# Splitting two pairs' projection weights early and reloading them as parts

## The chip, the cores and the metric

The kernel runs on one core of a Trainium2 chip. The time is that of one execution on the device, in microseconds (us); of several runs the median is given. One more execution was taken with the hardware profiler: its trace gives every instruction's start and duration on the engines PE (TensorE: matmuls and transposes), DVE (VectorE), ACT (ScalarE), POOL (GpSimd), and the transfers that SP (SyncE), ACT and POOL issue to the DMA engines.

## The reference

One decoder layer over 1024 positions of width 1024, in float32. Cut to what matters:

```python
hn = rms_norm(h, norm1_g[i])
proj = hn @ w_in[i]
a_b, a_c, a_h, q, k, v, c_u, c_v = jnp.split(proj, split_idx, axis=-1)
y_a = a_b * short_conv(a_c * a_h, conv_w[i])
q = rms_norm(q.reshape(bsz, s_len, ATTN_HEADS, HEAD_DIM), q_norm_g[i])   # 8 heads of 64
k = rms_norm(k.reshape(bsz, s_len, ATTN_HEADS, HEAD_DIM), k_norm_g[i])
y_b = stick_breaking_attention(q, k, v).reshape(bsz, s_len, ATTN_W)
y_c = spatial_gating(gelu(c_u), gelu(c_v), sgu_norm_g[i], sgu_w[i], sgu_b[i])
h = h + jnp.concatenate([y_a, y_b, y_c], axis=-1) @ w_out[i]
f = jnp.square(jax.nn.relu(rms_norm(h, norm2_g[i]) @ w_ff1[i]))
h = h + f @ w_ff2[i]
gate = jax.nn.sigmoid(rms_norm(h, norm3_g[i]) @ w_ple_gate[i])
h = h + gate * (p[i] @ w_ple_proj[i])
```

In `stick_breaking_attention` a position's weights come from a running product of `1 - sigmoid(z)` over the positions behind it.

## The kernel before

Products are float32 made from three matmuls of a faster type: every operand is split into a high part (`hi`, the operand rounded) and a low part (`lo`, the rest), and hi x hi, lo x hi and hi x lo are added up in PSUM (`product`, L157 to L164). A split (`split`, L131) is a CAST on ACT (L134) and a subtraction (L135) on DVE, or on POOL where `low` says so.

The stages follow one another: the product of `p` and the normalization of `x` (to about 45 us); the gating group's product vu and its work; then the eight attention heads, in four pairs. `project(pr)` makes q, k and v of pair `pr`. It takes eight weight tiles of 128 x 384 (k = 0 to 7), and for each of eight blocks of 128 positions (t) 24 matmuls 128 x 384 into one of two PSUM banks (`ps_mm`). A finished bank is read by a chain: the squares `qk_sq` on ACT (L376), their sum `ss` on DVE (L379), its power `rs` on POOL (L170), `qk` on DVE (L384), the high part of `V` on ACT and its low part on DVE; then the bank is free for t + 2. Later `qk_tr` (L403) transposes two blocks' `qk` on PE.

`load_w` (L141) loads one weight tile into a `stage` tile (seven of them) by an SP queue, and splits it into two tiles of the pool `wp`, which holds 20 (tag "w"). In `project` the low part is made on POOL for pairs 1 to 3 with even k, on DVE otherwise. `attend(pr)` makes the scores `z`, the scan `rem` (L457, DVE), the weights `wt` (L464, DVE or POOL), their transposes `w_tr` (L486) with the split `wT_hi`, `wT_lo`, and the product `av` (L504). Meanwhile DMAs of POOL (L305, accumulating) and ACT (L308, copying) form `w_sums` in DRAM, sums of blocks of a later stage's weights, and `y_both` and `y_dram` keep the attention's output (L435).

The main loop first runs `alone = stream(gating(), project(0))` by itself, the gating and project(0) in turn by fixed numbers of steps. Then it weaves the attention of pairs 0 to 3 with `fill = stream(project(1), project(2), project(3), convolve())`. The order on every engine is set by a scheduler at build time, from this order of writing and from buffers coming free. In the profiled execution project(0)'s matmuls start at 75.4 us, project(1)'s at 115.1, project(2)'s at 181.3, project(3)'s at 247. Behind them come the output projection, the two large products (L814) and the gate.

## Time and profile before

| | |
|---|---|
| median of 3 runs | 1207.83 us (1206.86 to 1211.2) |
| the profiled execution | 1206.75 us, its span 1205.0 us |
| granted TensorE clock in it | 0.997 |
| PE busy | 98% of the span |
| DVE, ACT, POOL busy | 73%, 49%, 33% |
| DMA, mean of the span | 211 GB/s |
| weight loads `stage<-in_w_qkv` | 32 of 192 KB |

The span runs from the first to the last instruction; the time holds some 1.75 us more. Busy time is summed over the span. In a row of a timeline the columns are start, duration, engine, line, operation, output and inputs, shape, and how often; in square brackets stands how long the engine was idle before it, and what ended that. Several instructions of one kind in a row are drawn together. PE's matmuls overlap, so what tells on PE is the distance of two starts.

### The profile page before, as it was taken

What the parts mean: (1) busy time and instruction counts of PE and PEld (TensorE: products, weight loads), DVE (VectorE), ACT (ScalarE), POOL (GpSimd) and SP (SyncE); (2) the same over time, 40 slices, a digit from 0 to 9 for tenths busy, and PEclk for the clock granted to TensorE, in tenths of its full rate; (3) what the DMA queues carried; (4) which work ended last, traced back from release to release, by engine and by line L of the source; (5) the groups of instructions that cost most, each with busy time, mean ns of one, the idle gap of its engine ahead of it and who ended that gap; (6) DMA issues with size and microseconds to landing.
All of it is one profiled execution on the core that took longest, in us unless ns stands there. A gap on an engine that the chain in (4) does not pass through costs nothing.

```text
span 1205.0 us, 17538 instructions
## 1 busy us (share of the span) xinstructions
PE 1181.0 (98%) x5788; PEld 1007.1 (84%) x5788; DVE 885.7 (73%) x1310; ACT 595.5 (49%) x1148; POOL 400.5 (33%) x472
## 2 busy tenths in 40 slices
PE   9999899998999999999999999999999999999997
PEld 7899899898888888888888888888888888888886
DVE  7846898989896667868877777787664657753697
ACT  7735565565643466733334333356543444456642
POOL 3324355464352222045354453421023301013412
PEclk9999999999999999999999999999999999999999
DMA  9602359999673776679998989777889975644857
GB/s 311 233 18 90 130 172 262 253 194 167 140 146 95 196 263 204 204 207 261 265 240 249 264 238 260 221 257 277 300 267 295 290 249 175 231 146 119 181 155 209
DMA packets 127963, 254.03 MB, mean 211 GB/s; under 512 B 14496, under 2 KB 22432, under 8 KB 127168
## 3 DMA queue, kind: packets, MB, share of 16 engines
q1 hardware_dynamic: 94992, 168.08, 41.4%
q0 software_dynamic: 27664, 57.05, 25.2%
q10 hardware_dynamic: 5216, 27.79, 6.4%
q8 instruction: 45, 0.74, 0.3%
q14 instruction: 46, 0.38, 0.1%
HBM read 192.30 MB, written 92.80 MB: 237 GB/s over the span
## 4 chain that ended last, share of the span: by engine, by line
PE 88%; DVE 8%; ACT 1%; issue 1%; DMA 1%; POOL 1%; SPq 0%; DVEq 0%; ACTq 0%; POOLq 0%
PE f_ps L814 25%; PE d_ps L814 25%; PE g_ps L814 6%; DVE rem L457 3%; PE qkv_ps L161 3%; PE qkv_ps L162 2%; PE qkv_ps L163 2%; PE o_ps L161 2%; PE o_ps L163 2%; PE o_ps L162 2%; PE av L504 2%; PE cv_ps L163 2%; PE cv_ps L161 2%; PE cv_ps L162 2%; PE w_tr L486 1%; PE vu_ps L162 1%
## 5 line engine op out<-in xcount | busy, mean ns | idle before, releaser
L135 DVE TENSOR_TENSOR w_lo<-raw,w_hi 128x512 fp32r<-128x512 f32 x280 | 243.1, 872 | 85.0 <-ACT w_hi L134 83.1
L134 ACT CAST w_hi<-raw 128x512 fp32r<-128x512 f32 x280 | 172.5, 620 | 240.5 <-PE d_ps L814 115.4
L814 PE MATMUL f_ps<-hn_hi,w_hi 128*128 128x512 f32 x448 | 175.2, 392 | 0.0
L814 PE MATMUL f_ps<-hn_lo,w_hi 128*128 128x512 f32 x448 | 174.9, 390 | 0.0
L814 PE MATMUL d_ps<-f_hi,w_hi 128*128 128x512 f32 x448 | 174.8, 390 | 0.0
L814 PE MATMUL f_ps<-hn_hi,w_lo 128*128 128x512 f32 x448 | 174.6, 391 | 0.0
L814 PE MATMUL d_ps<-f_hi,w_lo 128*128 128x512 f32 x448 | 174.3, 389 | 0.0
L814 PE MATMUL d_ps<-f_lo,w_hi 128*128 128x512 f32 x448 | 174.3, 389 | 0.0
L457 DVE TENSOR_TENSOR_SCAN rem<-rem,after 128x128 f32<-128x128 f32 (+3 forms) x64 | 90.9, 1431 | 13.3 <-ACT rem L452 13.3
L814 PEld LDWEIGHTS f_ps<-hn_lo,w_hi 128*128 128x128 f32 x448 | 84.5, 189 | 17.9 <-issue 0.2
L814 PEld LDWEIGHTS f_ps<-hn_hi,w_hi 128*128 128x128 f32 x448 | 84.5, 189 | 17.8 <-issue 0.2
L814 PEld LDWEIGHTS f_ps<-hn_hi,w_lo 128*128 128x128 f32 x448 | 84.5, 189 | 17.6
L814 PEld LDWEIGHTS d_ps<-f_hi,w_hi 128*128 128x128 f32 x448 | 84.1, 188 | 17.7 <-issue 0.2
L814 PEld LDWEIGHTS d_ps<-f_hi,w_lo 128*128 128x128 f32 x448 | 84.1, 188 | 17.6
L814 PEld LDWEIGHTS d_ps<-f_lo,w_hi 128*128 128x128 f32 x448 | 84.1, 188 | 17.5 <-issue 0.2
L161 PE MATMUL qkv_ps<-whi,xn_hi 128*128 128x384 f32 x256 | 88.8, 347 | 0.9 <-DVE V L138 0.8
L162 PE MATMUL qkv_ps<-wlo,xn_hi 128*128 128x384 f32 x256 | 86.6, 338 | 0.0
L163 PE MATMUL qkv_ps<-whi,xn_lo 128*128 128x384 f32 x256 | 86.3, 337 | 0.0
L135 DVE TENSOR_TENSOR f_lo<-raw,f_hi 128x512 fp32r<-128x512 f32 x112 | 78.2, 728 | 8.5 <-ACT f_hi L134 8.2
L134 ACT CAST f_hi<-raw 128x512 fp32r<-128x512 f32 x112 | 67.1, 620 | 25.6 <-DMA raw<-f_dram 21.6
L800 POOL TENSOR_TENSOR S<-S,sq 128x512 f32<-128x512 f32 x19 | 25.6, 1347 | 160.1 <-ACT sq L876 160.1
L452 ACT ACTIVATE rem<-z 128x128 f32<-128x128 f32 (+3 forms) x96 | 46.7, 500 | 24.3 <-PE z L450 21.6
(250 smaller groups left out, 2618.9 us busy)
## 6 DMA issues: line engine op xcount, KB each, us to landing
raw<-in_w_ff SPq DMA_DIRECT2D x148, 256.0 KB, 4.2
raw<-f_dram SPq DMA_DIRECT2D x112, 256.0 KB, 5.1
raw<-w_sums SPq DMA_DIRECT2D x64, 256.0 KB, 4.1
f_dram<-f SPq DMA_DIRECT2D x48, 256.0 KB, 3.9
f_dram<-t SPq DMA_DIRECT2D x48, 256.0 KB, 4.0
w_sums<-in_w_ff POOLq DMA_DIRECT2D x8, 1024.0 KB, 12.1
w_sums<-w_sums POOLq DMA_DIRECT2D x8, 1024.0 KB, 15.3
raw<-in_w_out SPq DMA_DIRECT2D x28, 256.0 KB, 3.5
```

The source lines that it names most:

```text
L134: last_hi[0] = nc.scalar.copy(hi, src)
L135: low.tensor_tensor(out=lo, in0=src, in1=hi, op=ALU.subtract)
L161: nc.tensor.matmul(ps, lh, rh, start=first and i == 0, stop=False)
L162: nc.tensor.matmul(ps, lh, rl, start=False, stop=False)
L163: done = nc.tensor.matmul(ps, ll, rh, start=False, stop=last and i == len(terms) - 1)
L452: last_act[0] = nc.scalar.activation(rem[:, ks], z, AF.Sigmoid, scale=-HD ** -0.5)
L457: nc.vector.tensor_tensor_scan(out=back, data0=back, data1=after[:, T - W:][:, ::-1], initial=1.0, op0=ALU.mult, op1=ALU.max)
L486: nc.tensor.transpose(tr[:, n:n + P], wts[i][:, kb * P:(kb + 1) * P], ident)
L504: nc.tensor.matmul(av[:, first * P:], lhs, part[:, o:o + m], start=kb == 0 and part is hi, stop=kb == 2 * g + 1 and part is lo)
L800: return eng.tensor_tensor(out=out, in0=x, in1=y, op=ALU.add)
L814: done = nc.tensor.matmul(bank, l, r, start=first and k == 0 and i == 0, stop=k == len(b) - 1 and i == 2, skip_group_check=True)
```

## The change

Project(0)'s weight loads are written at step 24 of `alone`. From its step 36 on, every fourth step makes one part: a weight tile of pair 1 or 2 is loaded (up to three ahead), split with its low part on DVE, and both parts are stored into `w_parts` in DRAM, the high part by ACT's queue and the low part by SP's. Project(1) and project(2) then load high and low parts by SP, without a split; seven of project(1)'s sixteen go into `stage` tiles, the others into `wp`. Project(3) loads and splits as before. Lines behind L345 move down by 36: L384 becomes L420, L457 L493, L464 L500.

```diff
+    w_parts = dram.tile([2, KT, 2, P, 384], F32, name="w_parts")
+    first_w, to_part = [], []
+
+    def load_first():
+        first_w.extend(load_w(a["w_qkv"][0, k], 384) for k in range(KT))
+
+    def part_weights(i):
+        while len(to_part) < min(i + 3, 2 * KT):
+            to_part.append(stage(a["w_qkv"][1 + len(to_part) // KT, len(to_part) % KT], 384))
+        hi, lo = (wp.tile([P, 384], F32R, tag="w", name=name(n)) for n in ("whi", "wlo"))
+        split(to_part[i], hi, lo)
+        to = w_parts[i // KT, i % KT]
+        nc.scalar.dma_start(to[0], hi.bitcast(F32))
+        nc.sync.dma_start(to[1], lo.bitcast(F32))
+
+    def parted_w(pr, k):
+        both = []
+        for part, n in enumerate(("whi", "wlo")):
+            if pr == 1 and 4 <= 2 * k + part < 4 + STAGES:
+                t = stp.tile([P, HT], F32R, tag="stage", name=name(n))[:, :384]
+            else:
+                t = wp.tile([P, 384], F32R, tag="w", name=name(n))
+            nc.sync.dma_start(t.bitcast(F32), w_parts[pr - 1, k, part])
+            both.append(t)
+        return both
+
     def project(pr):
 
-        wk = [load_w(a["w_qkv"][pr, k], 384, nc.gpsimd if pr and k % 2 == 0 else nc.vector)
-              for k in range(KT)]
+        if pr == 0:
+            wk = first_w
+        elif pr < 3:
+            wk = [parted_w(pr, k) for k in range(KT)]
+        else:
+            wk = [load_w(a["w_qkv"][pr, k], 384, nc.vector if k % 2 else nc.gpsimd)
+                  for k in range(KT)]
...
     alone = stream(gating(), project(0))
     fill = stream(project(1), project(2), project(3), convolve())
-    for _ in alone:
-        pass
+    for i, _ in enumerate(alone):
+        if i == 24:
+            load_first()
+        if i >= 36 and i % 4 == 0 and i // 4 - 9 < 2 * KT:
+            part_weights(i // 4 - 9)
```

The order of the instructions moves with it, at three places above all. A name's number only tells buffers apart; a row is line, operation, output and inputs, size.

On ACT, the end of the gating and project(0)'s first eviction (`qk_sq` from `qkv_ps`), before:

```order
L614 ACTIVATE v_sq_890<-vu_851 128x256
L375 COPY qk_sq_983<-ms_567 128x4
L375 COPY qk_sq_1020<-ms_567 128x4
L375 COPY qk_sq_1055<-ms_567 128x4
L590 COPY y_c_802<-c_tr_831 128x512
L590 COPY y_c_803<-c_tr_841 128x512
L134 CAST vn_734<-vu_851 128x4x64
L376 ACTIVATE qk_sq_983<-qkv_ps_958 128x4x64
```

and after:

```order
L650 ACTIVATE v_sq_1015<-vu_960 128x256
L134 CAST vn_803<-vu_960 128x4x64
L411 COPY qk_sq_1068<-ms_568 128x4
L411 COPY qk_sq_1113<-ms_568 128x4
L360 DMA w_parts<-whi_1303 128x384
L134 CAST whi_1356<-stage_1251 128x384
L626 COPY y_c_895<-c_tr_932 128x512
L411 COPY qk_sq_1156<-ms_568 128x4
L360 DMA w_parts<-whi_1356 128x384
L626 COPY y_c_896<-c_tr_942 128x512
L134 CAST vn_803<-vu_960 128x4x64
L412 ACTIVATE qk_sq_1068<-qkv_ps_1035 128x4x64
```

The last part's CAST and the last two parts' stores now stand just ahead of that eviction (the last row); the others stand further up among the gating's evictions. On DVE the sixteen `wlo` stand in the same stretch.

On DVE, the start of project(1), before:

```order
L384 TENSOR_TENSOR qk_1291<-qkv_ps_1249,rs_1289 128x256
L135 TENSOR_TENSOR wlo_1377<-stage_1374,whi_1376 128x384
L409 SCALAR_TENSOR_TENSOR KL_1152<-qk_tr_1274,c_gk,KH_1156 64x256
L409 SCALAR_TENSOR_TENSOR KL_1154<-qk_tr_1274,c_gk,KH_1156 64x256
L138 SCALAR_TENSOR_TENSOR V_1293<-qkv_ps_1249,r_731,V_1293 128x2x64
L135 TENSOR_TENSOR wlo_1389<-stage_1386,whi_1388 128x384
L135 TENSOR_TENSOR wlo_1401<-stage_1398,whi_1400 128x384
L379 TENSOR_REDUCE ss_1324<-qk_sq_1321 128x4
L457 SCALAR_TENSOR_TENSOR rem_1429<-rem_1429,after 128x384
L457 SCALAR_TENSOR_TENSOR rem_1444<-rem_1444,after 128x512
L464 TENSOR_TENSOR wt_1445<-rem_1444 128x511
L135 TENSOR_TENSOR wT_lo_1466<-w_tr_1461,wT_hi_1465 128x384
```

and after:

```order
L445 SCALAR_TENSOR_TENSOR KL_1269<-qk_tr_1403,c_gk,KH_1273 64x256
L445 SCALAR_TENSOR_TENSOR KL_1271<-qk_tr_1403,c_gk,KH_1273 64x256
L138 SCALAR_TENSOR_TENSOR V_1422<-qkv_ps_1378,r_800,V_1422 128x2x64
L415 TENSOR_REDUCE ss_1453<-qk_sq_1450 128x4
L493 SCALAR_TENSOR_TENSOR rem_1542<-rem_1542,after 128x384
L493 SCALAR_TENSOR_TENSOR rem_1557<-rem_1557,after 128x512
L420 TENSOR_TENSOR qk_1420<-qkv_ps_1425,rs_1455 128x256
L500 TENSOR_TENSOR wt_1558<-rem_1557 128x511
L138 SCALAR_TENSOR_TENSOR V_1422<-qkv_ps_1425,r_800,V_1422 128x2x64
L135 TENSOR_TENSOR wT_lo_1579<-w_tr_1574,wT_hi_1578 128x384
L415 TENSOR_REDUCE ss_1623<-qk_sq_1620 128x4
```

The three `wlo` ahead of `wT_lo` are gone; nothing else of the row moved but one `qk`, which stands ahead of `wt` now. POOL's four `wlo` of this stretch are gone too.

On DVE, the start of project(2), before (`wlo_3073` is the first of project(3)'s on DVE):

```order
L135 TENSOR_TENSOR wlo_2242<-stage_2239,whi_2241 128x384
L135 TENSOR_TENSOR wlo_2254<-stage_2251,whi_2253 128x384
L457 SCALAR_TENSOR_TENSOR rem_2163<-rem_2163,after 128x128
L457 SCALAR_TENSOR_TENSOR rem_2172<-rem_2172,after 128x256
L379 TENSOR_REDUCE ss_2202<-qk_sq_2199 128x4
L135 TENSOR_TENSOR wlo_3073<-stage_3070,whi_3072 128x384
L135 TENSOR_TENSOR wT_lo_2192<-w_tr_2187,wT_hi_2191 128x384
L457 SCALAR_TENSOR_TENSOR rem_2292<-rem_2292,after 128x384
L457 SCALAR_TENSOR_TENSOR rem_2307<-rem_2307,after 128x512
L464 TENSOR_TENSOR wt_2308<-rem_2307 128x511
L384 TENSOR_TENSOR qk_2110<-qkv_ps_2115,rs_2204 128x256
```

and after:

```order
L135 TENSOR_TENSOR wT_lo_2251<-w_tr_2246,wT_hi_2250 128x384
L493 SCALAR_TENSOR_TENSOR rem_2276<-rem_2276,after 128x128
L493 SCALAR_TENSOR_TENSOR rem_2285<-rem_2285,after 128x256
L135 TENSOR_TENSOR wlo_3170<-stage_3167,whi_3169 128x384
L415 TENSOR_REDUCE ss_2315<-qk_sq_2312 128x4
L135 TENSOR_TENSOR wT_lo_2305<-w_tr_2300,wT_hi_2304 128x384
L420 TENSOR_TENSOR qk_2223<-qkv_ps_2228,rs_2317 128x256
L493 SCALAR_TENSOR_TENSOR rem_2389<-rem_2389,after 128x384
L138 SCALAR_TENSOR_TENSOR V_2225<-qkv_ps_2228,r_800,V_2225 128x2x64
L493 SCALAR_TENSOR_TENSOR rem_2404<-rem_2404,after 128x512
L500 TENSOR_TENSOR wt_2405<-rem_2404 128x511
L135 TENSOR_TENSOR wT_lo_2426<-w_tr_2421,wT_hi_2425 128x384
```

`wlo_2242` and `wlo_2254` are gone and project(3)'s `wlo_3170` has stayed; `qk` of project(1)'s last block (the last row before, the seventh now) stands ahead of the scans of 384 and 512 and of `wt`.

On PE, the last product of project(2)'s first block and the second block around it, after:

```order
L163 MATMUL qkv_ps_2466<-whi_2334,xn_lo_299 128x384
L522 MATMUL w_tr_2494<-ident,wt_2390 128x128
L161 MATMUL qkv_ps_2466<-whi_2338,xn_hi_331 128x384
L162 MATMUL qkv_ps_2466<-wlo_2340,xn_hi_331 128x384
L163 MATMUL qkv_ps_2466<-whi_2338,xn_lo_332 128x384
L522 MATMUL w_tr_2494<-ident,wt_2405 128x128
L162 MATMUL qkv_ps_2363<-wlo_2352,xn_hi_430 128x384
L163 MATMUL qkv_ps_2363<-whi_2350,xn_lo_431 128x384
```

In the order of before the first block's k = 7 products stand together ahead of the second block's. Now its lo product waits for `wlo_2352` behind five of the second block's eight k. That tile's load stands on SP behind stage loads of pair 3:

```order
L372 DMA wlo_2344<-w_parts 128x384
L372 DMA whi_2346<-w_parts 128x384
L372 DMA wlo_2348<-w_parts 128x384
L372 DMA whi_2350<-w_parts 128x384
L67 DMA stage_3161<-in_w_qkv 128x384
L67 DMA stage_3167<-in_w_qkv 128x384
L67 DMA stage_3173<-in_w_qkv 128x384
L67 DMA stage_3179<-in_w_qkv 128x384
L67 DMA stage_3185<-in_w_qkv 128x384
L372 DMA wlo_2352<-w_parts 128x384
L67 DMA stage_3191<-in_w_qkv 128x384
L67 DMA stage_3197<-in_w_qkv 128x384
```

Before, the tiles of pair 2 were all loaded ahead of any of pair 3.

## The prediction

> **What bounds the kernel now.** I read the page first, then TensorE's waits, then the stages by windows, and then the timelines around the two long waits. The rows are engine, line, tile, the engine waited for, total, times and longest in the second part of the fence.
>
> ```profile
> span 1205.0 us, 17538 instructions
> PE 1181.0 (98%) x5788; PEld 1007.1 (84%) x5788; DVE 885.7 (73%) x1310; ACT 595.5 (49%) x1148; POOL 400.5 (33%) x472
> ...
> PE w_tr L486 <- DVE KL L409: 3.6, 4, 1.5
> PE w_tr L486 <- DVE wt L464: 3.2, 3, 1.6
> PE av L504 <- DVE wT_lo L135: 2.9, 4, 1.8
> PE qk_tr L403 <- DVE qk L384: 1.5, 1, 1.5
> ```
>
> PE is busy 98% of the span, so the change can win only what PE waits; the change takes no matmul away. The waits named here are all on DVE and sum to 11.2 us. Only those can go whose DVE queue holds weight splits, so I look by stage (columns: window, length, then PE, DVE, ACT, POOL busy; clock; DMA share; GB/s).
>
> ```profile
> 53.00:80.00 27.00, 27.00 (x139) 23.44 (x138) 13.39 (x40) 9.36 (x22) 8.24 (x11) 1.00 0.14 46
> 111.00:122.00 11.00, 9.24 (x57) 8.85 (x56) 10.71 (x17) 6.80 (x20) 8.78 (x11) 1.00 0.67 241
> 122.00:138.00 16.00, 16.00 (x100) 15.71 (x99) 10.72 (x20) 9.10 (x24) 6.28 (x9) 1.00 0.66 213
> 138.00:166.00 28.00, 24.58 (x157) 22.02 (x156) 27.25 (x35) 15.55 (x38) 9.74 (x13) 1.00 0.21 76
> 174.00:190.00 16.00, 14.53 (x100) 13.79 (x98) 15.64 (x24) 10.05 (x28) 15.05 (x23) 1.00 0.97 227
> 190.00:205.00 15.00, 15.00 (x93) 14.70 (x93) 10.51 (x19) 8.46 (x22) 5.67 (x9) 1.00 0.91 274
> ```
>
> DVE is full in 111–122, 138–166 and 174–190. Splits of pair 1's and pair 2's weights stand in the first and the last of these; 138–166 is full of scans alone. Between the first two DVE has 5.3 us free of 16, so no backlog of the first reaches the second. The stage in which the change puts the splits, 53–80, has DVE half free, ACT two thirds free and the DMA engines almost empty.
>
> **Part 1: the splits at project(1)'s start go.** The wait there, and what DVE and POOL do ahead of it:
>
> ```profile
> 121.43 0.38 PE L504 MATMUL av<-wT_lo,V 128*128 128x256 f32 x1 [1.76 <-DVE wT_lo L135]
> ...
> 112.84 0.55 DVE L135 TENSOR_TENSOR wlo<-stage,whi 128x384 fp32r<-128x384 f32 x1
> ...
> 114.59 2.35 DVE L135 TENSOR_TENSOR wlo<-stage,whi 128x384 fp32r<-128x384 f32 x2
> ...
> 112.94 4.87 POOL L135 TENSOR_TENSOR wlo<-stage,whi 128x384 fp32r<-128x384 f32 x4
> ```
>
> From 111.2 on DVE runs without a gap to wT_lo. The three wlo ahead of it take 0.55 + 2.35 = 2.90 us of that; without them wT_lo could end up to 2.9 us sooner, more than the 1.76 that PE waited. Gain: 1.76, with 0 (if scan and cast ahead of wT_lo come no sooner) as the other end. I take the whole, because DVE shows no idle time in that stretch.
>
> **Part 2: three of the four wlo on DVE around project(2)'s start go.**
>
> ```profile
> 189.06 0.44 PE L403 MATMUL qk_tr<-ident,qk 128*128 128x128 f32 x2 [1.47 <-DVE qk L384]
> ...
> 178.46 4.09 DVE L135 TENSOR_TENSOR wlo<-stage,whi 128x384 fp32r<-128x384 f32 x2
> ...
> 183.71 1.35 DVE L135 TENSOR_TENSOR wlo<-stage,whi 128x384 fp32r<-128x384 f32 x1
> ...
> 188.59 0.41 DVE L384 TENSOR_TENSOR qk<-qkv_ps,rs 128x256 f32<-128x256 f32 x1
> ...
> 178.78 3.35 POOL L135 TENSOR_TENSOR wlo<-stage,whi 128x384 fp32r<-128x384 f32 x2
> ```
>
> The 4.09 us of the pair at 178.46 go (and one more at 175.26). The one at 183.71 belongs to pair 3 and stays. In the new order qk also stands ahead of the two scans and the wt that preceded it. 4.09 us is more than the wait, so the gain is 1.47; its lower end is again 0. Upper end of both parts together: all the time by which DVE's queue is shortened, 2.90 + 4.09 = 7.0, which PE can use only where it waits; the waits of 138–166 have no split ahead of them, so I give them nothing. Sum of gains: 3.2 us.
>
> **Part 3: the 16 parts in 52–80.** Added per part: one CAST on ACT, one lo on DVE, one store issued by ACT, one by SP, and one load (192 KB each, moved from later). Their rows (mean ns of one is the last figure ahead of the idle time; issue rows: ns min/median/max; loads and stores: median us to landing):
>
> ```profile
> L134 ACT CAST whi<-stage 128x384 fp32r<-128x384 f32 (+1 forms) x56 | 27.0, 497 | 3.6 <-DMA stage<-in_w_conv 2.0 <-DMA stage<-in_w_qkv 0.5 <-PE qkv_ps L162 0.5
> L135 DVE TENSOR_TENSOR wlo<-stage,whi 128x384 fp32r<-128x384 f32 (+1 forms) x44 | 30.7, 711 | 1.3 <-ACT whi L134 0.6 <-PE cv_ps L163 0.6
> ...
> L308 ACTq DMA_DIRECT2D w_sums<-in_w_ff x16: 496/512/611, 115.0 to 232.2; - x16
> ...
> y_dram<-y_c SPq DMA_DIRECT2D x2, 256.0 KB, 2.0
> ...
> stage<-in_w_qkv SPq DMA_DIRECT2D x12, 192.0 KB, 3.0
> ...
> f_dram<-f SPq DMA_DIRECT2D x48, 256.0 KB, 3.9
> ```
>
> DVE: 16 x 0.71 = 11.4 us beside 13.4 busy of 27: fits. ACT: 16 x (0.50 + 0.51) = 16.1 us beside 9.4: 25.5 of 27 plus what is left until 82, so it fits with little over. PE does not depend on the parts themselves, but the evictions of the gating and of project(0) stand behind them in ACT's and DVE's queues.
>
> The pool has 20 tiles and project(0)'s weights hold 16, so four are left: the hi and lo of two parts. A part's CAST therefore waits until the stores two parts back have landed. One turn of the ring makes two parts and takes a CAST, 0.5, the landing of the store, and what stands between in ACT's queue, on average 9.4/16 = 0.6. The landing is not in this stage's rows. Its ends are 2.0 (y_dram, in this quiet stage) and 3.9 (f_dram, in the up-projection). Weight loads at 40–54 took 3.0. The traffic gives a floor: six transfers of 192 KB a turn are 1.18 MB, and the fastest stretch of the trace moved
>
> ```profile
> DMA packets 4134, 9.06 MB, mean 362 GB/s; under 512 B 507, under 2 KB 732, under 8 KB 4132
> ```
>
> (9–34 us), thus 3.3 us a turn. I take a landing of 2.7, nearest the 3.0, and a turn of 3.8. The last two of the three CASTs at 51.31 (51.8 and 52.3) are pair 1's and become the first two parts; seven turns follow, and the last CAST must be done before project(0)'s first eviction:
>
> ```profile
> 51.31 1.54 ACT L134 CAST whi<-stage 128x384 fp32r<-128x384 f32 x3 [0.51 <-DMA stage<-in_w_qkv]
> ...
> 80.67 0.39 ACT L376 ACTIVATE qk_sq<-qkv_ps 128x256 f32<-128x256 f32 x1 [0.79 <-PE qkv_ps L163]
> ...
> 83.56 0.35 DVE L138 SCALAR_TENSOR_TENSOR V<-qkv_ps,r,V 128x128 fp32r<-128x128 f32 x1 [0.44 <-ACT V L137]
> ...
> 85.48 0.42 PE L161 MATMUL qkv_ps<-whi,xn_hi 128*128 128x384 f32 x1
> 85.74 0.34 PE L162 MATMUL qkv_ps<-wlo,xn_hi 128*128 128x384 f32 x1
> 85.92 0.33 PE L163 MATMUL qkv_ps<-whi,xn_lo 128*128 128x384 f32 x1
> ```
>
> The eviction that starts at 80.67 ends on DVE at 83.91, and its bank, one of two, is needed for t = 2 at 85.48: it can slip 1.57 us, to 82.2. The last CAST starts at 52.4 + 7 x 3.8 = 79.0. Cost 0, with 2.7 us to spare. With a turn of 0.5 + 3.9 + 0.6 = 5.0 it starts at 87.4, ends at 87.9, and PE loses 5.7 us; that is the upper end. The turn at which the loss begins is 4.2, a landing of 3.1.
>
> The Trainium skill ("DMA: Bandwidth & Descriptors", "Anatomy of one DMA") fits a transfer as 2.0 us and its bytes at 436 GB/s; by that a store of 192 KB would land in 2.45 us as an estimate, the ring would be clear of the eviction, and the sum would stay as it is. The same page ("Latency and other measured facts") speaks against the change: it names the memory's latency as most of the fixed cost and gives it as 0.2 us on average but 2 us at high load. By that the landing would grow with the very traffic that the parts bring. The trace agrees in direction (2.0 for stores here at 46 GB/s, 3.9 for those of the up-projection); this case is the second rival below.
>
> **Part 4: the weights come back as parts.** SP issues 32 loads instead of 16 for these two pairs. For pair 1 eleven come in project(0)'s time, where PE reads other tiles: 0. Five wait for project(0)'s last eight-step product, which ends in 114; the last is issued at about 111 and read at about 118 (project(1) starts at 115). Loads of that stretch landed in 9.0 median (third row below), most of them behind w_sums copies that start at 115; by that row PE would lose 2 us, by the 3.0 above nothing. I take 0, for they are issued ahead of the copies. Eleven of pair 2's follow and have 60 us: 0. Pair 2's last five wait for project(1)'s last matmuls, and the very last, k = 7's lo (wlo_2352), stands behind five stage loads of pair 3.
>
> ```profile
> 179.64 0.33 PE L161 MATMUL qkv_ps<-whi,xn_hi 128*128 128x384 f32 x1
> ...
> 186.59 0.42 PE L161 MATMUL qkv_ps<-whi,xn_hi 128*128 128x384 f32 x1
> ...
> stage<-in_w_qkv SPq DMA_DIRECT2D x7, 192.0 KB, 9.0
> ...
> stage<-in_w_qkv SPq DMA_DIRECT2D x7, 192.0 KB, 15.0
> ...
> DMA to landing us min/median/max: 2.4/14.9/16.9
> ```
>
> The k = 7 matmuls of project(1)'s t = 7 start at 179.64, or 177.9 once part 1's gain is taken off, so the load is issued at 177 to 179. PE meets wlo_2352 after t = 0's hi of k = 7 (before: 186.59; now 184.8), six short matmuls, fifteen of t = 1 at 0.18 (85.74 to 85.92 above) and two transposes: about 189. That leaves 10 to 12 us. Loads of 174–202 landed in 15.0 median (fourth row; all loads of that line in the last), while two accumulating transfers of w_sums shared the DMA engines; the first landed in 2.4. wlo_2352 stands between, behind five loads: I take 11 and cost it 0.7 us, with ends 0 and 5 (15 us from 179 is 194).
>
> **Sum.** 1206.75 (the profiled execution: span 1205.0 and 1.75 around it) - 1.76 - 1.47 + 0 + 0.7 = 1204.2. The profiled run lies 1.1 below the median of the runs, 1207.83; since the runs spread up to 1211.2 I put the forecast between the two scales, at 1204.8.
>
> **Rivals.**
> 1. *The stalls only move.* wlo_2352 lands by the median of 15, or pair 3's first two loads, for whose CAST ACT waits in order, come as late. Then part 2's gain is eaten and PE waits on the load: 1206.75 - 3.2 + 5 = 1208.5, or, where only a gain falls out, 1206. For it: the 15.0 row. Against it: the five loads ahead of it are issued before the accumulating transfers are under way.
> 2. *Slower: the ring of four tiles.* The landing rises under the ring's own traffic. At 3.9 it costs 5.7 us, and the time is 1206.75 - 3.2 + 0.7 + 5.7 = 1210; at the 5.9 us that 256 KB loads took in 9–34 with the engines full, the turn is 7.0, the last CAST ends at 101.9, PE loses up to 19.7 and the time is 1224. It decides from a landing of about 3.6: there 7 x 0.5 = 3.5 us are lost, all the gain.
>
> ```profile
> stage<-in_xT SPq DMA_DIRECT2D x15, 256.0 KB, 5.9
> ```
>
>    Against it: at most four stores and three loads are under way, and a slow landing thins out the traffic that makes it slow.
> 3. *More gain.* DVE works 0.55 to 2 us on one wlo where POOL has wlo too; without POOL's splits the scans beside them would run shorter, and every one of the 11.2 us of waits might shrink: 1206.75 - 7.0 = 1199.7. Against it: most of the rest stands in 138–166 and after 205, where there is no split.
>
> **How the numbers follow.** Forecast 0.55 (1203 to 1206.5), stalls move 0.20 (1206 to 1209), ring 0.16 (1208 to 1224), more gain 0.09 (1199 to 1203). 8 times in 10 is held by 1202 to 1212: it leaves out most of the third rival and the upper half of the ring's. About 0.5%, 6 us, is what a measurement of this kernel can tell from no change. Faster by that needs 1201.8: 0.08. Slower by that needs 1213.9: 0.09. The rest, 0.83, is no change that can be told.
>
> **What would show it.** Right: the waits at 121.4 and 189.1 are gone, PE's waits <-DVE wT_lo and <-DVE qk shrink, those <-DVE KL and <-DVE wt stay; w_parts stores land in 2.5 to 3; the last w_parts CAST starts by 80; project(0)'s evictions have no wait ahead of them. Wrong: PE waits for qkv_ps or vu_ps behind ACT around 80–90 (the ring), for a DMA into wlo near 189 (the late part), or waits at 121 and 189 that keep their size under another name.

## The result: slower by 0.67%, and the profile after

| | before | after |
|---|---|---|
| median | 1208.34 us (4 runs, 1206.86 to 1211.2) | 1215.64 us (4 runs, 1215.4 to 1218.68) |
| ratio after / before, 95% interval | | 1.0067 [1.0052, 1.0081] |
| profiled execution, its span | 1206.75, 1205.0 | 1215.74, 1214.0 |

The forecast was 1204.8 with a range of 1202 to 1212: wrong, and on the wrong side. Ratios are taken over fast executions alone; one of 3058.64 us (the run without the accumulating transfers) and one of 1398.20 us (the first of the two runs under "Together") are left out below. The page of the changed kernel and TensorE's waits in it (engine, line, tile, the engine waited for; total, times, longest):

```profile
span 1214.0 us, 17680 instructions
PE 1187.5 (98%) x5788; PEld 1012.3 (83%) x5788; DVE 887.0 (73%) x1318; ACT 594.9 (49%) x1148; POOL 394.0 (32%) x464
...
PE w_tr L522 <- DVE KL L445: 4.1, 4, 1.6
PE w_tr L522 <- DVE wt L500: 1.8, 2, 1.0
PE z L484 <- DVE QS L454: 1.7, 1, 1.7
PE qkv_ps L162 <- DMA wlo<-w_parts: 1.6, 1, 1.6
PE qk_tr L439 <- DVE qk L420: 1.5, 2, 1.1
```

PE has 5788 matmuls as before, and the wait on `wT_lo` has fallen from 2.9 to 0.2 us. The five longest waits are together no longer than the four before (10.7 and 11.2 us), yet the span is 9.0 us longer: the waits are not where all of the loss shows, since slow matmuls and matmuls between two short waits count as busy. So I set the start of each block t of each project(pr) (its first matmul) beside the same matmul before:

| start of | before, us | after, us | after minus before |
|---|---|---|---|
| project(0), t = 0 | 75.37 | 75.36 | -0.01 |
| project(0), t = 2 | 85.48 | 89.22 | +3.74 |
| project(0), t = 3 | 90.61 | 95.56 | +4.95 |
| project(1), t = 0 | 115.14 | 120.07 | +4.94 |
| project(1), t = 1 | 122.75 | 125.10 | +2.35 |
| project(2), t = 0 | 181.32 | 184.18 | +2.86 |
| project(2), t = 1 | 190.16 | 193.66 | +3.50 |
| project(2), t = 2 | 196.25 | 204.78 | +8.52 |
| start of the last matmul | 1196.35 | 1205.32 | +8.96 |

There are three places: a loss of 4.95 us at 80 to 95, a gain of 2.1 us by project(2)'s start, a loss of 5.7 us at 184 to 205. Behind them the difference swings by up to 2 us and ends 0.4 us higher. PE's order is not quite the old one: some six of the attention's short matmuls have changed sides at project(1)'s t = 1 and at project(2)'s t = 0 and t = 1, so these rows hold about 1 us that is order and not time. Where the same matmuls stand ahead of a block, at project(1)'s t = 5 (+2.59), and nearly so at project(2)'s t = 3 (+8.29, two matmuls off), the loss between is 5.7 us again.

**The first place, the ring.** The stage by windows (columns as in the prediction), and the DMA queues in 55 to 85 us (packets, MB, share of the 16 engines; then the issues with KB of one and median us to landing):

```profile
53.00:62.00 9.00, 9.00 (x45) 7.57 (x44) 6.23 (x18) 4.89 (x11) 2.02 (x2) 1.00 0.93 306
62.00:71.00 9.00, 9.00 (x45) 7.56 (x43) 5.70 (x18) 4.03 (x9) 2.01 (x2) 1.00 0.95 303
71.00:80.00 9.00, 8.37 (x47) 7.07 (x46) 5.15 (x15) 4.43 (x10) 1.20 (x3) 1.00 0.89 286
```

```profile
DMA packets 6643, 9.10 MB, mean 303 GB/s; under 512 B 736, under 2 KB 6641, under 8 KB 6641
...
q1 hardware_dynamic: 4536, 6.21, 66.3%
q10 hardware_dynamic: 2105, 2.87, 27.7%
...
w_parts<-wlo SPq DMA_DIRECT2D x16, 192.0 KB, 3.1
w_parts<-whi ACTq DMA_DIRECT2D x14, 192.0 KB, 3.3
stage<-in_w_qkv SPq DMA_DIRECT2D x9, 192.0 KB, 3.7
whi<-w_parts SPq DMA_DIRECT2D x3, 192.0 KB, 3.9
wlo<-w_parts SPq DMA_DIRECT2D x3, 192.0 KB, 3.9
y_dram<-y_c SPq DMA_DIRECT2D x1, 256.0 KB, 3.3
```

Neither DVE nor ACT is full, as the prediction said, but the DMA engines are: 0.14 of them were busy before in this stage, now 0.89 to 0.95, and they move only 303 GB/s. ACT's timeline shows, of the sixteen CASTs, the second and then the last two that had to wait for a store, and behind them project(0)'s first eviction:

```profile
53.77 0.50 ACT L134 CAST whi<-stage 128x384 fp32r<-128x384 f32 x1
...
78.01 0.51 ACT L134 CAST whi<-stage 128x384 fp32r<-128x384 f32 x1 [2.24 <-DMA w_parts<-whi]
...
82.88 0.51 ACT L134 CAST whi<-stage 128x384 fp32r<-128x384 f32 x1 [1.72 <-DMA w_parts<-whi]
...
83.30 0.58 ACT L626 COPY y_c<-c_tr 128x512 f32<-128x512 f32 x1
...
83.87 0.59 ACT L626 COPY y_c<-c_tr 128x512 f32<-128x512 f32 x1
85.49 0.41 ACT L134 CAST vn<-vu 128x256 fp32r<-128x256 f32 x1 [1.03 <-DVE vu L660]
85.80 0.38 ACT L412 ACTIVATE qk_sq<-qkv_ps 128x256 f32<-128x256 f32 x1
```

From the second part's CAST at 53.77 to the sixteenth's at 82.88 are seven turns of 4.16 us. Behind the last CAST stand two copies and a CAST of the gating, and the eviction starts at 85.80, where it started at 80.67 before; 1.57 us of these 5.13 were free. The last link runs over DVE: the CAST of `vn` at 85.49 waited for it, and DVE had stood at the last part's `wlo`, whose tile was still being stored:

```profile
84.10 0.56 DVE L135 TENSOR_TENSOR wlo<-stage,whi 128x384 fp32r<-128x384 f32 x1 [0.78 <-DMA w_parts<-wlo]
84.58 0.42 DVE L658 TENSOR_TENSOR vu<-vu,vrs 128x256 f32<-128x256 f32 x1
85.03 0.42 DVE L660 TENSOR_TENSOR vu<-vu,gs_b 128x256 f32<-128x256 f32 x1
```

On PE:

```profile
88.35 0.61 PE L439 MATMUL qk_tr<-ident,qk 128*128 128x128 f32 x2 [1.09 <-DVE qk L420]
89.22 0.66 PE L161 MATMUL qkv_ps<-whi,xn_hi 128*128 128x384 f32 x1 [0.27 <-DVE V L138]
89.68 0.52 PE L162 MATMUL qkv_ps<-wlo,xn_hi 128*128 128x384 f32 x1
90.00 0.52 PE L163 MATMUL qkv_ps<-whi,xn_lo 128*128 128x384 f32 x1
```

The starts at 89.68 and 90.00 are 0.32 us apart, where 0.18 was usual. Two windows tell why:

```profile
85.00:88.00 3.00, 2.08 (x11) 1.36 (x10) 1.31 (x4) 0.89 (x3) 1.58 (x3) 1.00 1.02 359
88.00:91.00 3.00, 2.39 (x8) 2.02 (x9) 2.00 (x7) 0.84 (x3) 1.00 (x1) 0.58 0.92 302
```

The granted clock (the third figure from the end) is 0.58 in the second. The clock's record in the trace has a half-clock stretch of 3.41 us from 88.48 on, after PE had been busy for only 2.08 of the 3 us from 85 to 88. It adds the last 1.2 us to the 3.74.

**The second place, the late tile.** ACT, DVE, PE and the issuing engines, 179 to 200 us:

```profile
179.32 2.16 POOL L305 DMA_DIRECT2D w_sums<-in_w_ff  x2
...
184.12 0.54 SPq L372 DMA_DIRECT2D wlo<-w_parts  x1
...
189.40 0.51 ACT L134 CAST whi<-stage 128x384 fp32r<-128x384 f32 x1 [3.24 <-PE qkv_ps L163]
...
189.94 0.56 DVE L135 TENSOR_TENSOR wlo<-stage,whi 128x384 fp32r<-128x384 f32 x1 [5.68 <-ACT whi L134]
...
193.66 0.41 PE L161 MATMUL qkv_ps<-whi,xn_hi 128*128 128x384 f32 x1 [0.76 <-DVE V L138]
...
199.92 0.45 PE L162 MATMUL qkv_ps<-wlo,xn_hi 128*128 128x384 f32 x1 [1.62 <-DMA wlo<-w_parts]
```

The last part of pair 2 (wlo_2352) is issued at 184.12, lands at 199.88 and is read at 199.92. Ahead of that ACT waits for pair 3's second weight load (it landed at 189.32, the CAST starts at 189.40; PE, which the bracket names, had been done long), and DVE stands 5.68 us behind that CAST. PE waits at 193.66 for a bank of project(1) that came free late through this. The two waits overlap; which of them bounds is a question for the runs.

### The profile page after: what moved, and what is told of

Same layout as the page of the kernel before. It is cut to its first block, busy times and chain, and to the rows that moved or that the text cites. A ratio compares the mean times of both kernels' runs of the same rounds, so it can differ in the third digit from the quotient of the medians.

```text
span 1214.0 us, 17680 instructions
## 1 busy us (share of the span) xinstructions
PE 1187.5 (98%) x5788; PEld 1012.3 (83%) x5788; DVE 887.0 (73%) x1318; ACT 594.9 (49%) x1148; POOL 394.0 (32%) x464
## 4 chain that ended last, share of the span: by engine, by line
PE 86%; DVE 6%; DMA 4%; ACT 1%; POOL 1%; issue 1%; SPq 0%; ACTq 0%; DVEq 0%; POOLq 0%
PE f_ps L853 25%; PE d_ps L853 25%; PE g_ps L853 6%; PE qkv_ps L161 3%; PE qkv_ps L162 3%; PE qkv_ps L163 3%; DVE rem L493 2%; PE o_ps L161 2%; PE o_ps L162 2%; PE o_ps L163 2%; PE av L540 2%; PE w_tr L522 2%; PE cv_ps L163 2%; PE cv_ps L162 2%; DMA w_parts<-whi 2%; PE cv_ps L161 2%
## 5 line engine op out<-in xcount | busy, mean ns | idle before, releaser
L493 DVE TENSOR_TENSOR_SCAN rem<-rem,after 128x128 f32<-128x128 f32 (+3 forms) x64 | 90.3, 1422 | 13.5 <-ACT rem L488 13.1
L170 POOL TENSOR_TENSOR rs<-ss,mhalf 128x4 f32<-128x4 f32 x32 | 39.1, 1221 | 76.9 <-DVE ss L415 76.9
```

Source lines behind the costliest of these rows:

```text
L170: last_power[0] = nc.gpsimd.tensor_tensor(out=out, in0=in_, in1=mhalf[:, :n], op=ALU.pow)
L493: nc.vector.tensor_tensor_scan(out=back, data0=back, data1=after[:, T - W:][:, ::-1], initial=1.0, op0=ALU.mult, op1=ALU.max)
```

## The experiments

All are made from the changed kernel unless the text says otherwise. Only the lines that matter are shown; `evicted` collects each block's first eviction (`qk_sq`) and, under its own key, the last part's load, and `made` counts the parts. Ratios are to the kernel before, on the same chip.

**The ring.** Three ways to relieve it. First the parts of pair 2 are spread over project(0)'s time, each queued on ACT behind an eviction:

```diff
-        if i >= 36 and i % 4 == 0 and i // 4 - 9 < 2 * KT:
-            part_weights(i // 4 - 9)
+        if made[0] < KT and i >= 36 and i % 4 == 0:
+            part_weights(made[0])
+            made[0] += 1
+        if KT <= made[0] < 2 * KT and evicted and i % 2 == 0:
+            with tc.issue_after(list(evicted.values())[-1].ins):
+                part_weights(made[0])
+                made[0] += 1
```

> Pair 1's eight parts stay in the gating; pair 2's eight are queued on ACT behind project(0)'s evictions. If the ring of four tiles is what costs (evictions of project(0) late by 3.7 us, then 1.2 us at a halved TensorE clock), the waits at 76 to 90 and the slow clock at 88 go and the time falls by 4 to 5 us, to about 1211; the loss at 184 to 205 stays. If the parts cost wherever they stand (their traffic, ACT's issues), at least 3 us of it come back in project(0) and the time is 1213 or more.

Measured: 1209.26 us, 1.0012 [0.9999, 1.0026]. Project(0)'s t = 3 starts 0.05 us after that of before, project(1) 0.68 after. So the ring's loss goes when the parts are spread, and 6.4 of the 7.3 us go with it: better than the 4 to 5 us expected, for the second place costs less here too (3.5 us from project(1)'s t = 4 to project(2)'s t = 4). What stays: at project(2) PE still waits 3.27 us for a wlo of w_parts.

Then six more tiles for the ring, with the same parts and transfers: every third part is made in tiles that are free in this stage.

```diff
+        if i % 3 == 2:
+            hi, lo = (slot(n, F32R)[:, :384] for n in ("whi", "wlo"))
+        else:
+            hi, lo = (wp.tile([P, 384], F32R, tag="w", name=name(n)) for n in ("whi", "wlo"))
-        hi, lo = (wp.tile([P, 384], F32R, tag="w", name=name(n)) for n in ("whi", "wlo"))
```

> Every third part is made in a pair of slot tiles, so six more tiles than four serve the stores at once; the traffic is the same. If the number of tiles is what holds the parts (a CAST waits for a landing, turn 4 us for two parts), the casts come about a third faster, the last of those ahead of project(0) by 75, and the wait at 85 to 89 goes: 1211. If the DMA engines are full (95% busy, 303 GB/s at 55 to 85), landings grow instead, the casts keep a pace of about 2 us, and at least 2 us of the 5 stay: 1213 to 1216.

And less traffic with the same four tiles: all 16 parts are split from the first three loaded tiles (13 loads left out, so pairs 1 and 2 get other weights).

```diff
-        while len(to_part) < min(i + 3, 2 * KT):
+        while len(to_part) < 3:
-        split(to_part[i], hi, lo)
+        split(to_part[i % 3], hi, lo)
```

> All sixteen parts are split from the first three weight tiles, so thirteen loads of 192 KB are left out (two pairs get repeated weights); ring, CASTs and stores stay. If traffic holds the parts, two transfers a part in place of three at 303 GB/s allow a turn of 2.6 us, landings fall to 2.5 us, the last CAST comes before 76 and the 5 us at 76 to 95 go: 1210.5. If the ring's fixed landing and ACT's order hold them, the turn stays at 3.5 us or more and at least 2 us of the loss remain.

Measured: 1212.88 us, 1.0032 [1.002, 1.0044] with six tiles; 1216.71 us, 1.0063 [1.0046, 1.008] with fewer loads. The issues of 55 to 85 us in the run with fewer loads:

```profile
w_parts<-wlo SPq DMA_DIRECT2D x15, 192.0 KB, 2.4
w_parts<-whi ACTq DMA_DIRECT2D x14, 192.0 KB, 2.5
```

Stores land in 2.4 and 2.5 us instead of 3.1 and 3.3, the last CAST starts at 75.74, and project(1) starts 0.56 us after that of before. With six tiles it starts 0.22 ahead. Either cure takes the ring's loss away, but neither went wholly as expected. With fewer loads a turn takes 3.14 us (53.73 to 75.74), where 2.6 was expected. With six tiles thirteen parts are cast by 73.30, at 1.87 us each from the second on (52.69), hardly faster than the 1.95 of the changed kernel's first thirteen (53.77 to 75.25). The other three come at 80.03, 84.35 and 95.89, the last two behind project(0)'s first eviction at 81.56. So that run changes the place of three parts as well as the number of tiles, and the pace says that the place did more. Less traffic alone is shown to be enough; more tiles alone are not. In both runs PE is then ahead: project(2)'s t = 1 starts 4.27 us (six tiles) and 3.35 us (fewer loads) ahead of that of before; counted by matmuls done, PE is 2.95 and 2.04 us ahead there. And in both the lead is lost at the next block, and with it the times that were expected (1211 and 1210.5). PE with six tiles:

```profile
195.78 0.69 PE L162 MATMUL qkv_ps<-wlo,xn_hi 128*128 128x384 f32 x1 [6.79 <-DMA wlo<-w_parts]
```

With fewer loads it waits 6.5 us at the same place. The sooner PE arrives, the longer it waits there.

**The late tile.** First pair 3's CASTs on ACT are held until project(2)'s second eviction, so that ACT does not wait for pair 3's loads:

```diff
+            with tc.issue_after(evicted[2, 1].ins):
+                wk = [load_w(a["w_qkv"][pr, k], 384, nc.vector if k % 2 else nc.gpsimd)
+                      for k in range(KT)]
```

> Pair 3's CASTs are queued on ACT behind project(2)'s second eviction; the loads and their order stay. If ACT and DVE blocked behind these CASTs are the bound at 184 to 205, 5 us go: 1210 to 1211. If the late tile wlo_2352 is (it landed at 199.9), DVE's 5.7 us of idle time go, but PE only comes sooner to that tile and waits there: 1214 to 1216.

Measured: 1217.54 us, 1.007 [1.0055, 1.0085], above even the range expected if the tile is the bound. DVE's stand behind that CAST is gone, and the time is not better. PE's first wait is now:

```profile
PE qkv_ps L162 <- DMA wlo<-w_parts: 8.6, 1, 8.6
```

The tile, issued at 183.99, lands at 202.22, and ACT's copies into w_sums, issued 4 us sooner than in the changed kernel (188.34), are under way beside it. So the tile is the bound, and ACT's wait in the changed kernel only hid a part of it.

Then pair 3's loads are queued on SP behind wlo_2352 instead of ahead of it:

```diff
+            evicted["last part"] = nc.sync.dma_start(t.bitcast(F32), w_parts[pr - 1, k, part])
-            nc.sync.dma_start(t.bitcast(F32), w_parts[pr - 1, k, part])
...
+            with tc.issue_after(evicted["last part"].ins):
+                wk = [load_w(a["w_qkv"][pr, k], 384, nc.vector if k % 2 else nc.gpsimd)
+                      for k in range(KT)]
```

> On SP's queue pair 3's stage loads are put behind wlo_2352; the order on ACT and DVE follows by itself, with pair 3's CASTs some ten rows later. If the order of this queue makes both the tile and the block, wlo_2352 lands within 8 us and the 5.7 us at 184 to 205 go: about 1210.5. If the accumulating transfers delay any load there, wlo_2352 still lands 12 us or more after its issue, and at most 1 to 2 us go.

Measured: 1210.91 us, 1.0023 [1.0008, 1.0038], with the ring's loss still in it. The tile lands 7.6 us after its issue (186.84 to 194.40) instead of 15.8, and project(2)'s t = 0 to t = 2 lose 2.5 us instead of 5.7. The profiled execution took 1216.93 us, 6 more than the median, so I read no more from it.

Last, the two accumulating transfers of w_sums that start at 179 are left out, and with them a part of those sums:

```diff
+                if what[0] == "+" and i == 6:
+                    continue
```

> The two accumulating transfers of w_sums at about 179 us are left out (the sums of one block step lack them), nothing else. If their traffic makes the loads late, all loads there land in 3 to 5 us, DVE's 5.7 us of idle time and the wait for wlo_2352 go, and the time is 1209 to 1211. If the queue's order alone makes them late, it stays within 1 us of 1215.6.

Measured: 1211.55 us, 1.0021 [1.0008, 1.0033]; 1209 to 1211 was expected. The issues at 172 to 206 us:

```profile
stage<-in_w_qkv SPq DMA_DIRECT2D x8, 192.0 KB, 3.6
wlo<-w_parts SPq DMA_DIRECT2D x3, 192.0 KB, 3.1
```

In the changed kernel the eight stage loads took 12.2 us in the median; here 3.6, and wlo_2352 5.4 (182.96 to 188.39). So most of the landing of 15.8 us is made by the accumulating transfers; the five loads ahead of the tile cost it some 3 us without them, and about 8 beside them (15.8 here, 7.6 with the tile queued first). Project(2)'s t = 2 then starts 2.27 us after that of before instead of 8.52. But the profiled execution gives 4.1 us back in one wait on `KL` that ends at 222.76, with a stretch of half clock from 220.00 on. What that wait is comes further down.

**Together.** The parts spread and pair 3's loads behind the last part; then also the accumulating transfers one step later:

```diff
-            block_sums(i, (last_pool[0], last_act[0]))
+            if i != 6:
+                block_sums(i, (last_pool[0], last_act[0]))
+            if i == 7:
+                block_sums(6, (last_pool[0], last_act[0]))
```

> Both edits together: pair 2's parts behind project(0)'s evictions, and pair 3's loads behind wlo_2352 on SP. If the loss was those two places and nothing else, what is left is the gain at project(1) and project(2): 2 to 4 us under the kernel before, 1204.5 to 1207, with no wait of PE for a w_parts load. If the accumulating transfers, which the spread kernel issued ahead of pair 2's last part loads, still hold these up, wlo_2352 lands at 186 or later, PE waits 1 to 3 us for it, and the time is that of before, 1207 to 1210.

> As spread_last, and the two accumulating transfers of that block step are issued one step of attention (about 7 us) later, so pair 2's last loads go ahead of them. If these transfers delay the loads, wlo_2352 lands within 5 us of its issue and the time is 1 to 3 us under spread_last, 1203 to 1206. If they only shift the crowding to pair 3's loads and w_sums copies, it is within 1 us of spread_last.

Measured: 1210.90 us, 1.0025 [1.0016, 1.0034], and 1209.43 us, 1.0012 [1.0, 1.0024]; the first is above both ranges expected, the second neither at 1203 to 1206 nor within 1 us of the first. In the first PE no longer waits for the tile, which lands 7.5 us after its issue (178.28 to 185.81), but for `wT_hi` on ACT (1.17) and `QS` on DVE (1.73). In the second the tile lands in 2.3 us (180.22 to 182.55), and little is won: six of pair 3's eight loads, queued behind it, now land at 194.9 to 207.3, and PE waits for `y_both` on ACT (2.2) and for `wT_hi` (1.8) instead (its profiled execution took 1213.35 us, 3.9 more than the median).

The parts spread with both holds, pair 3's loads and its CASTs:

```diff
+            with tc.issue_after(evicted["last part"].ins), tc.issue_after(evicted[2, 1].ins):
```

> The spread kernel with both holds: pair 3's loads behind wlo_2352 on SP and pair 3's CASTs behind project(2)'s second eviction on ACT. If spread_last lost to the ACT queue standing at pair 3's CASTs for late loads (waits of 1.2 and 1.7 us on ACT and QS at 190 to 196), these waits go: 2 to 3 us under spread_last, about 1208 to 1209. If they are set by the w_parts load of that time, no change from 1211.

Measured: 1208.96 us, 1.001 [1.0002, 1.0019], in the range expected if ACT's queue was the bound. But the two waits that were to go still stand: PE waits at 192.85 for `wT_hi` on ACT (1.27) and at 197.15 for `QS` on DVE (1.23). So the time came out as expected and the reason given for it is not shown. No wait for w_parts is left at project(2).

Only pair 1 in parts, one every eight steps, pair 2 split in place as before:

```diff
-        while len(to_part) < min(i + 3, 2 * KT):
+        while len(to_part) < min(i + 3, KT):
-            if pr == 1 and 4 <= 2 * k + part < 4 + STAGES:
+            if False:
-        elif pr < 3:
+        elif pr == 1:
-        if i >= 36 and i % 4 == 0 and i // 4 - 9 < 2 * KT:
-            part_weights(i // 4 - 9)
+        if i >= 36 and i % 8 == 4 and i // 8 - 4 < KT:
+            part_weights(i // 8 - 4)
```

> Only pair 1's weights are made as parts, one every eight steps; its 16 loads go to weight tiles alone, pair 2 and 3 are split in place as before. If four ring tiles suffice at half the rate, project(0) starts its evictions on time, and part 1's gain of 1.8 us is kept: 1206 to 1208, unless PE waits in project(1)'s first product for the twelve loads that now come after project(0), which would cost 1 to 4 us and end at 1208 to 1211.

Measured: 1213.49 us, 1.0039 [1.0024, 1.0055], above everything expected. The ring costs only 0.54 us, but without the stage tiles as targets the parts come too late for project(1) (PE waits 1.94 us for a wlo at 121.80), and the order of the attention behind it changes. Pair 1 alone is thus no gain either; the run does not single out a cost.

**What the gains are worth.** The kernel before, with pairs 1 and 2 using pair 0's weights: their 16 loads and splits are left out, and no part is made. This is parts 1 and 2 of the prediction without any of the costs.

```diff
-        wk = [load_w(a["w_qkv"][pr, k], 384, nc.gpsimd if pr and k % 2 == 0 else nc.vector)
-              for k in range(KT)]
+        if pr in (1, 2):
+            wk = kept_w[0]
+        else:
+            wk = [load_w(a["w_qkv"][pr, k], 384, nc.gpsimd if pr and k % 2 == 0 else nc.vector)
+                  for k in range(KT)]
+            kept_w.append(wk)
```

> The kernel before, with pair 1 and pair 2 multiplied by pair 0's weights, which stay in their tiles: their 16 loads and 16 splits are left out and nothing takes their place. It is the most that any placing of these splits can win. If the two waits at 121 and 189 are won whole, as the prediction's sum has it, 3 to 4 us: about 1205. If the waits come back elsewhere (other DVE work, the conveyance of the attention), under 1.5 us: 1207 or more.

Measured: 1208.25 us, 1.0001 [0.9992, 1.001]: nothing is won. Yet the gains are there at first: project(1)'s t = 2 starts 2.28 us and project(2)'s t = 3 3.20 us ahead of that of before, with the same matmuls ahead of each. At project(2)'s t = 4 it is a lag of 1.33. One wait takes it. PE and DVE there:

```profile
217.58 1.09 PE L490 MATMUL w_tr<-ident,wt 128*128 128x128 f32 x4 [4.01 <-DVE KL L413]
...
210.57 2.02 DVE L461 TENSOR_TENSOR_SCAN rem<-rem,after 128x896 f32<-128x896 f32 x1
212.50 0.40 DVE L388 TENSOR_TENSOR qk<-qkv_ps,rs 128x256 f32<-128x256 f32 x1
212.81 3.74 DVE L461 TENSOR_TENSOR_SCAN rem<-rem,after 128x1024 f32<-128x1024 f32 x1
216.48 0.95 DVE L413 SCALAR_TENSOR_TENSOR KL<-qk_tr,c_gk,KH 64x256 fp32r<-64x256 f32 x2
```

And in the kernel before:

```profile
216.36 0.63 PE L486 MATMUL w_tr<-ident,wt 128*128 128x128 f32 x4 [0.86 <-DVE KL L409]
...
213.33 2.01 DVE L457 TENSOR_TENSOR_SCAN rem<-rem,after 128x896 f32<-128x896 f32 x1
215.26 0.96 DVE L409 SCALAR_TENSOR_TENSOR KL<-qk_tr,c_gk,KH 64x256 fp32r<-64x256 f32 x2
...
216.85 2.46 DVE L457 TENSOR_TENSOR_SCAN rem<-rem,after 128x1024 f32<-128x1024 f32 x1
```

DVE is full in both (without a gap from 205.45 to 221 in this run, 12.79 of 13 us busy at 205 to 218 before). But a full DVE did not take the lead: the scan of 896 starts 2.76 us sooner than before. What differs is the order. Before, `KL` follows that scan at once, and the scan of 1024 comes after it; in this run the scheduler has put `qk` and the scan of 1024, which took 3.74 us here, ahead of `KL`. Had `KL` followed the scan of 896 here too, it would have started at about 212.50 and not at 216.48 (an estimate from these rows), and PE would hardly have waited. The same turned order, with the same 3.74 us, stands at the wait of 4.1 us in the run without the accumulating transfers; in the changed kernel and in the runs with six tiles `KL` stands ahead of that scan. So this run shows that the two waits can be removed and that the end need not move, but not what they are worth with the order kept: no run holds it.

The last run puts the pieces together with all the traffic kept: six more tiles, pair 3's loads behind the last part, its CASTs behind project(2)'s second eviction (the diffs above).

> The changed kernel with six more tiles for the parts (every third part is made in other tiles), and pair 3's loads queued on SP behind the last part's load, their CASTs on ACT behind project(2)'s second eviction; so the ring's loss and the late tile are both taken on, with all the traffic kept. Theory (ring and late tile are the only losses, and the gains of parts 1 and 2 are given back behind 205 as with the 16 loads left out): PE stands some 3 us ahead of the kernel before at project(2)'s start, the last part's tile lands within 8 us of its issue, the wait for it at 190 to 196 is under 1.5 us, a wait on KL or wt of 2 us or more stands behind 205, and the time is 1207.5 to 1209.5. Rival (the gain is kept once both losses are gone): no such wait behind 205, 1204 to 1206. Second rival (the accumulating transfers of w_sums, not the order of the loads, make the tile late): it lands over 12 us behind its issue again, PE waits 4 us or more for it, 1211 to 1213.

Measured: 1207.60 us against 1208.02, 0.9998 [0.9986, 1.001]. With both losses taken on and all the traffic kept, nothing of the slowdown is left that the measurement can tell. The time is in the range of the first theory, but by luck as to the gains: the theory had them given back behind 205, and no wait of 2 us stands there. The lead (2.9 us by matmuls done at project(2)'s t = 1) is spent by t = 2, where 0.22 is left. The rival by which the gain is kept falls for this kernel. The tile landed 8.1 us after its issue (177.45 to 185.57) and PE does not wait for it; it waits here:

```profile
191.32 0.38 PE L545 MATMUL av<-wT_hi,V 128*128 128x256 f32 x1 [1.35 <-ACT y_both L554]
...
194.32 0.30 PE L489 MATMUL z<-KH,QS 128*128 128x128 f32 x1 [0.69 <-DVE QS L459]
...
185.59 4.51 ACTq L308 DMA_DIRECT2D w_sums<-in_w_ff  x2
190.15 0.47 ACT L137 ACTIVATE QS<-qk_tr,c_gq 128x256 fp32r<-128x256 f32 x1 [6.00 <-DMA stage<-in_w_qkv]
```

These two waits are 2.04 of the 2.7 us. ACT, with no CAST of pair 3 in its way, stands 6.0 us behind its own two copies into w_sums: the first is issued at 185.59, when the last part's tile has landed (185.57), the second at 189.61, when a stage load of pair 3 has landed (189.59).

## Why the prediction was wrong, step by step

**The steps that failed are two cost terms: Part 3's 0, which measured 4.95 us, and Part 4's 0.7, which measured 5.66.** Together they are more than the whole miss.

**Parts 1 and 2, the gains: right in size, kept in no run.** Where the same matmuls stand ahead, the changed kernel gains 2.06 us from project(1)'s t = 0 to t = 2 (+4.94 to +2.88; 1.76 forecast). Part 2's gain is covered by the late tile there; with the 16 loads and splits left out both together are 2.98 us (from 0.22 ahead at project(1)'s start to 3.20 at project(2)'s t = 3; 3.23 forecast). The sum carried them through to the end of the run, and in no run did they last: once they went in a wait that a changed order on DVE made, once in waits behind ACT's own copies. Whether they would last with the order kept stays open. The third rival (more gain) is not borne out: no lead at a block with the same matmuls ahead of it was over 3.2 us, against its 7.0.

**Part 3, the ring: the mechanism was on record as the second rival, but the path behind the last CAST was not costed.** Three terms were off. The turn was 4.16 us, not 3.8: seven turns took 2.5 us more. The second part started at 53.77, 1.4 us later than put. And from the start of the last CAST to the eviction the prediction had only the CAST's 0.5 us, where the new order, quoted ahead of it, has two `y_c` copies and the CAST of `vn` between: 2.9 us (82.88 to 85.80), 1.03 of them a wait for DVE, which stood at the last `wlo`. The prediction had named DVE's queue and costed ACT's alone. 2.5 + 1.4 + 2.4 is 6.3 us against the 2.7 to spare, so 3.6 us too late; PE shows 3.74 at t = 2. The landing was 3.1 and 3.3, not 2.7; but a turn of 4.16 is still inside the threshold of 4.2, so by the prediction's own sum it would have cost nothing. It was the other two terms that made it a loss.

The floor of the turn was too low. It was put at 3.3 us from 362 GB/s, read in a stage whose packets are larger (9.06 MB in 4134; here 9.10 MB in 6643). By the rows above, the 46 transfers listed for 55 to 85 us took 94% of 30 us: 0.61 us each with all engines, six of them 3.7 us (an estimate from these rows). So the traffic accounts for most of the 4.16: with two transfers a part in place of three the turn fell to 3.14, and with six more tiles but all the transfers two parts still took 3.75. The argument that "a slow landing thins out the traffic" named the balance that was reached, not a reason for a short landing. The cost: 3.74 us, and 1.2 more in the half clock that followed, against an upper end of 5.7.

The Trainium skill ("DMA: Bandwidth & Descriptors", "Anatomy of one DMA") gives 2.45 us for such a store as an estimate, by a fit that the page made for transfers issued by POOL; the trace agrees where 13 loads were left out (2.4 and 2.5) and not in the full ring (3.1 and 3.3). The same page ("Latency and other measured facts") has the latency rise with load, and here the trace agrees.

**Part 4, the loads of parts: 0 for pair 1 was right** (no wait for w_parts at project(1) in the changed kernel); **0.7 us for wlo_2352 was mis-sized.** The issue was put at 177 to 179; it came at 184.12, for project(1) ended 3 us later through the ring, and the load went out only when project(1)'s last matmul had ended (183.99). The landing was 15.8, not 11. The upper end of 5 us was near: project(2)'s t = 0 to t = 2 lost 5.66. What spoke "against" the rival, that the five loads ahead are issued before the accumulating transfers are under way, was false: those were issued at 179.32 and 180.07, the five loads from 179.71. The first rival had both doors, the tile and ACT's CASTs for pair 3; the runs show the tile as the bound.

**The sum as it came.** 4.95 (ring) - 2.08 (gain to project(2)'s start) + 5.66 (late tile) + 0.44 (the rest) = 8.97, the profiled difference. The median's is 7.3. Taken away one at a time the losses are not additive: without the ring 6.4 us of 7.3 go, with the tile earlier 4.7, with both 4.7 (1210.90), and with both and six tiles in place of the spread all of it. In the runs looked at, PE's next waits are then on the attention's work on ACT and DVE, between 190 and 223.

**Open.** What the two gains are worth when DVE's order behind 205 is held as it was; no run held it. Why the accumulating transfers slow other queues that much was not tried, only that they do. No version beat the kernel before by more than the measurement can tell; the best, six tiles with both holds, equals it.

## What to carry to other kernels

A wait that is removed is worth only what is left of it at the end: before costing the removal, leave the work out altogether (nothing in its place) and see whether the end moves. Where it does not, find the one place at which the lead goes, and compare the order of the instructions there with the order before: a scheduler that sets the order anew can take the lead by turning two rows round, and then the run says nothing of the removal itself. When a chain of added work is to fit ahead of a deadline, cost what stands between its last step and the deadline in the new order, on every engine that the chain uses. A ring of few buffers through DRAM turns hardly faster than the DMA traffic that it makes itself allows: count all transfers of a turn at the price that such packets have, and take the landing under that load, not that of a quiet stage. When loads are moved, look at which transfer is last in its queue and what large transfers of other queues start just then.

## What the runs showed of the hardware

- **A short stop of PE can cost as much again in clock.** In the changed kernel PE was busy for 2.08 of 3 us in 85 to 88, and a stretch of half clock of 3.41 us followed. The stretches that began at 88.48, 194.29, 225.01 and 525.38 lie on one grid: they are 31, 9 and 88 times 3.413 us apart. Not every window with such stops was followed by one, and the threshold stays open; nor does the clock add up one to one: the stretch at 88.48 cost 1.2 us, and that at 225.01 nothing (project(2)'s t = 4 is 8.55 us late and its t = 5 8.56). The Trainium skill ("TensorE: Matmul & The Clock Gate", "Part 1: The HAM clock gate (the "warmup" mystery)") has the free-running window of 3413 ns and the half rate, and the trace agrees; it speaks of an idle window, and here PE was idle in part of it only.
- **Accumulating transfers hold up the loads beside them.** Two of 1 MB each on POOL's queue raise the median landing of 192 KB loads on SP's from 3.6 to 12.2 us.
- **Queues wait on each other's landings.** In the trace each transfer names the semaphore that it sets. Transfers of SP and ACT take eight of them in turn, and one is issued only when the transfer that had its semaphore before has landed. In the last run ACT's copy at 189.61 sets the one that SP's stage load held until 189.59; in the changed kernel the copy at 193.14 follows a stage load that landed at 193.12; in the kernel before one at 188.06 follows one of 188.04. So a late load on SP seems able to stop ACT's compute, which no buffer ties to it. This is read from the semaphores and the coincidences; no run tested it.
- **A scan can run long.** The DVE scan of 1024 took 2.28 to 2.46 us in most places, 2.80 at 225.05 in the changed kernel, 3.74 at 212.81 with the weights left out, and 3.74 again at 218.00 without the accumulating transfers. Its cause was not looked into.
